# Layer 0's modulation by narrow float32 matmuls on TensorE, with another order of its weight tiles

## The chip, the core and the metric

The kernel runs on one core of one Trainium2 chip. The metric is the device time of one execution in microseconds; the runs of a kernel are given by their median. Times inside an execution are counted from the start of the profile's span.

## What is computed

Two layers on 256 tokens of width 1024. A condition vector c gives six vectors per layer (shift, scale and gate, twice); layer 0's are called SH1, SC1, G1, SH2, SC2, G2 here.

```python
cond = jax.nn.silu(c)
for l in range(DEPTH):
    mod = (cond @ w_ada[l] + b_ada[l])[:, None, :]
    sh1, sc1, g1, sh2, sc2, g2 = jnp.split(mod, N_MOD, axis=-1)
    h = rms_norm(x, norm1_g[l]) * (1.0 + sc1) + sh1
    proj = h @ w_in[l]
    ...
    y = rms_norm(y, jnp.ones((MIX_WIDTH // 2,), jnp.float32)).reshape(B, S, MIX_WIDTH) * mix_norm_g[l]
    x = x + g1 * (y @ w_out[l])
    h2 = rms_norm(x, norm2_g[l]) * (1.0 + sc2) + sh2
    x = x + g2 * peer_ffn(h2, peer_wq[l], peer_subkeys[l], peer_u[l], peer_v[l])
```

Between proj and y stand a pooling over windows and a sliding-window attention with normed queries and keys. `w_ada[l]` is 1024 x 6144 in float32, so each of the six vectors takes eight tiles of 128 x 1024 (512 KB).

## The kernel before

A layer has a mixer (`mixer`) and an expert part (`peer`). All weights come as tiles of 128 x 1024 float32 through one list, `items`, in the order of their use. `Stream` loads them on SP's queue (line 81), up to nine items ahead, into five buffers `rawt`, or for items marked so into the five buffers `hlt` of the splits. A load waits until the last reader of its buffer is done, and the queue is in order: what stands behind a waiting load waits too. Tiles of the large products are split into two float16 parts, the first by ScalarE (line 86), the second by VectorE (line 87).

The framework's scheduler puts each engine's instructions in an order when the program is built. `high_priority` and `issue_after` in the code shift that order.

Modulation of layer 0, before: `ada_step` takes a tile and accumulates cond[k] * tile in a [128, 1024] buffer on VectorE (lines 285 and 287). For G1 ScalarE scales the tile in its buffer (line 281) and GpSimd adds it (line 283). After eight tiles a product with ones sums over the partitions: `ada_cols` gives columns (line 261, eight matmuls), the gate's row is spread over all partitions by line 298. SC1 and SH1 stand first in `items`, then the ten tiles of w_in, then G1, w_out, SC2 and SH2 mixed.

The mixer of layer 0: row factors of x's norm (line 373 and `rsqrt`, lines 231 to 236), turns of x on TensorE by a diagonal of the factors (line 357 makes the diagonal, line 360 turns, four per PSUM tile), scale and shift (line 387), split into `hbuf` (lines 351, 352). Then the projection with w_in (lines 319 and 309; line 478 sums squares for the Q/K norm, line 500 spreads its factors), scores (516), probabilities turned (544), attention product (554), pooling (595 to 609). `y_half` norms each half of y and turns it (line 360 again). The output projection `mm_v` (line 327) multiplies y's two float16 parts with w_out's: six matmuls of 512 columns for each of eight slices and two token tiles, 96 in all. `residuals` multiplies by the gate, adds to x and starts the second norm; its turns come last, and behind them the first query product of the expert part (line 319).

PSUM has eight banks: two `mm`, four `acc`, two `g`. The output projection's two token tiles need two `acc` banks each.

Of the kernel before, what the change touches and what calls it, by code (L numbers as in the profile page):

```python
# [23 lines left out]
L = 2  # L24
# [21 lines left out]
class Arena:  # L46
    """Hands out column ranges of one float32 tile."""
# [15 lines left out]
class Stream:  # L63
    """Weight tiles [128, 1024] in the order of their use; loads and splits run ahead.  An item with a
    fourth field is loaded into a buffer of the splits."""
# [36 lines left out]
    def get(self, kind):  # L102
        """The next tile: (hi, lo), or the raw tile where the item has no scale."""
        i = self.at
        assert self.items[i][2] == kind, (self.items[i][2], kind)
        self._dma(i + self.ad)
        self._conv(i + self.ac)
        self.at += 1
        return self.ct.pop(i) if self.items[i][1] is not None else self.rt.pop(i)

    def advance(self, ahead=None):
        """Splits that were held back by limit."""
        self.limit = len(self.items)
        self._conv(self.at + (self.ac if ahead is None else ahead))
# [6 lines left out]
def trunk(ctx, tc, ins, out):  # L121
# [56 lines left out]
    def spread(main, bg, lo, hi):  # L178
        """bg spread evenly between main[lo:hi]."""
# [11 lines left out]

    items = []
    items += ada_rows(0, SC1) + ada_rows(0, SH1)
    items += conv_items(ins["win"][0], 10, None, "pre")
    vend = [0, 0]
    late = [t + (True,) for t in ada_rows(0, SC2)]
    for n, pair in enumerate(zip(ada_rows(0, G1), conv_items(ins["wout"][0], 8, None, "pre"))):
        items += [*pair, late[n]] if n < NSC else pair
    for n, t in enumerate(ada_rows(0, SH2)):
        items += [t, late[n]] if n >= NSC else [t]  # L200
# [39 lines left out]
    def load_exp_tables():  # L240
        """The set with ln and exp, behind the last activation that needs another one."""
# [7 lines left out]
    def mod_finish(l, c, src, j0, n):  # L249
        """mod columns from c*W: + bias, and for the scales (1 + .) * norm gain."""  # L250
# [51 lines left out]

    def mm_u(pt, w, hi, lo):
        """pt[128 columns of w, T] = w^T h over the 8 slices of the contraction."""
# [7 lines left out]
    def mm_u2(ws, hi, lo):  # L312
        """Two such products side by side, so that the slices of h are wanted at half the pace."""
# [8 lines left out]
    def mm_v(acc, w, ahi, alo, first, end):  # L322
        """acc[half][128 t, 512] += a^T w for one contraction tile and one tile of tokens."""
# [12 lines left out]
    def residuals(product, accs, grow, tmp, norm, extra):  # L336
        """product(tt), which ends accs[tt], then x += grow * accs, and the norm of x."""
# [16 lines left out]
    def transposes(pts, src, r, ks, tt):  # L354
        """Slices ks of token tile tt of src, rows scaled by r, transposed into pts, two slices each."""
# [7 lines left out]
    class Norm:  # L363
        """RMS norm of x over D, affine per column, transposed and split into hhi/hlo."""
# [4 lines left out]
        def tile(self, tt):  # L369
            """The row factors of token tile tt."""  # L370
# [22 lines left out]
    def take_pre(n):  # L393
        """Splits the next n tiles of the stream into act's first columns, before their use."""
# [6 lines left out]
    # ---------------------------------------------------------------- attention  # L401
    def mixer(l, norm):
# [36 lines left out]
        if l == 0:  # L439
            norm = Norm()  # L440
            rs = [norm.tile(tt) for tt in range(2)]
            for n in range(TAT):
                ada_step(None, None, acc_a if n < 8 else grow1)
            with tc.issue_after(last["ada"]):
                ada_cols(0, SC1, acc_a, pacc())
                for tt in range(2):
                    norm.turn(tt, rs[tt])
            for _ in range(16 - TAT):
                ada_step(pacc, None, grow1)
# [36 lines left out]
        # q: chunk c holds head c (partitions 0-63) and head 4+c (64-127)  # L486
# [75 lines left out]
        # pooling: the channel mix first, then the window means less the token, a banded product  # L562
# [11 lines left out]
        def y_half(h):  # L574
            """Group norm of one half of y, transposed, scaled and split."""
# [38 lines left out]
        if l == 0:  # L614
            acch = act[:, PRE:PRE + 1024]
            st.limit = st.at + 31
            nh = 0
            while st.at <= st.limit:
                if st.kind() == "pre":
                    take_pre(1)  # L620
                elif st.kind()[2] == G1:
                    ada_step(pmm, {G1: grow1}, grow1, True)
                elif st.kind()[2] == SH2:
                    ada_step(None, None, acch, nh < NPOOL)
                    nh += 1
                else:
                    ada_step(None)
# [5 lines left out]
        for k in range(4):  # L633
            w = pre.pop(0)
            for tt in range(2):
                mm_v(accs[tt], w, hhi[:, k, tok[tt]], hlo[:, k, tok[tt]], k == 0, False)
        ws = [pre.pop(0) for _ in range(4)]
        st.advance(4)

        def rest(tt):  # L640
            for k in range(4, 8):
                mm_v(accs[tt], ws[k - 4], hhi[:, k, tok[tt]], hlo[:, k, tok[tt]], False, k == 7)

        def extra():
            if l == 0:
                ada_cols(0, SH2, acch, pacc())
                ada_cols(0, SC2, acc_a, pacc())
# [5 lines left out]
    # ---------------------------------------------------------------- experts  # L653

    def peer(l):
# [16 lines left out]
        def picks():  # L672
            """Top-k and what follows from it, in steps of about a microsecond of the vector engine."""
# [31 lines left out]
            # gates: softmax of the picked scores, the first of which is the largest  # L705
# [3 lines left out]
            # candidate number -> (a, b)  # L709
# [48 lines left out]
        def gates():  # L758
            """act *= gate matrix, for expert columns [64 r, 64 r + 64), 8 tokens at a time."""
# [30 lines left out]
        # queries and key scores  # L790
# [45 lines left out]
        # product with V  # L836
# [57 lines left out]
def layout(inputs):  # L894
    """Host side: the inputs laid out for contiguous loads, and constants of the shapes."""
# [5 lines left out]
    def u_like(w):  # L901
        """[L, 1024, n*128] -> [L, n, 128 p, 8 k * 128 c]"""
# [3 lines left out]
    def colform(b):  # L906
        """[L, m*128] -> [128, L, m]"""
# [62 lines left out]
```

## Time and profile before

| | us |
|---|---|
| runs, median of 3 | 1781.52 |
| runs, lowest and highest | 1780.1, 1783.76 |
| profiled execution, span | 1780.2 |
| TensorE busy in it | 1705.0 |
| VectorE busy in it | 1436.6 |
| ScalarE busy in it | 852.5 |

The profile gives the span, from the first to the last instruction of one execution; the runs are whole device times, and the profiled execution has no other time of its own than its span. The mean granted clock of TensorE over the span is 0.985. The views name an instruction by its line, engine, operation, output tile and input tiles. A float32 matmul appears as two passes, so counts of float32 groups are twice those of the code. The modelled end of a matmul lies behind the start of the next one, so the distance of starts tells the pace.

### The profile page before, as it was taken

What the parts mean: (1) busy time and instruction counts of PE and PEld (TensorE: products, weight loads), DVE (VectorE), ACT (ScalarE), POOL (GpSimd) and SP (SyncE); (2) the same over time, 40 slices, a digit from 0 to 9 for tenths busy, and PEclk for the clock granted to TensorE, in tenths of its full rate; (3) what the DMA queues carried; (4) which work ended last, traced back from release to release, by engine and by line L of the source; (5) the groups of instructions that cost most, each with busy time, mean ns of one, the idle gap of its engine ahead of it and who ended that gap; (6) DMA issues with size and microseconds to landing.
All of it is one profiled execution on the core that took longest, in us unless ns stands there. A gap on an engine that the chain in (4) does not pass through costs nothing.

```text
span 1780.2 us, 33654 instructions
## 1 busy us (share of the span) xinstructions
PE 1705.0 (96%) x13524; PEld 1212.5 (68%) x13524; DVE 1436.6 (81%) x2587; ACT 852.5 (48%) x1146; POOL 29.2 (2%) x26
## 2 busy tenths in 40 slices
PE   4999989999999999999999998999999999999998
PEld 3758868999997455444458697888999845454443
DVE  6797999578889999877867499945888899986664
ACT  3645544544444444445656353545444444445543
POOL 0210000000000000000000000000000000000000
PEclk9989999999999999999999999999999999999999
DMA  8773456776665555778844144565555555556773
GB/s 315 285 277 120 168 196 220 264 241 207 222 220 187 187 190 199 257 259 314 315 155 154 36 152 163 180 220 201 187 181 188 186 181 183 185 189 213 227 227 126
DMA packets 100190, 364.04 MB, mean 204 GB/s; under 512 B 11680, under 2 KB 11696, under 8 KB 99648
## 3 DMA queue, kind: packets, MB, share of 16 engines
q1 hardware_dynamic: 99648, 361.29, 59.0%
q8 instruction: 106, 1.74, 0.4%
q0 software_dynamic: 384, 0.58, 0.1%
q14 instruction: 52, 0.43, 0.1%
HBM read 360.78 MB, written 1.05 MB: 203 GB/s over the span
## 4 chain that ended last, share of the span: by engine, by line
PE 81%; DVE 13%; DMA 2%; ACT 2%; issue 2%; SPq 0%; DVEq 0%; ACTq 0%
PE acc L327 38%; PE mm L309 34%; DVE hlt L87 4%; PE g L778 2%; PE g L780 2%; DVE act L670 1%; DVE act L668 1%; DVE act L667 1%; DVE act L669 1%; PE acc L319 1%; DMA rawt<-in_wq_dram 1%; DVE act L666 1%; DMA rawt<-in_adar_dram 1%; PE acc L516 1%; PE g L554 1%
## 5 line engine op out<-in xcount | busy, mean ns | idle before, releaser
L309 PE MATMUL mm<-hbuf,hlt 128*128 128x256 f16 x6816 | 767.5, 273 | 20.6 <-ACT act L828 11.1
L86 ACT ACTIVATE hlt<-rawt 128x1024 f16<-128x1024 f32 x544 | 571.4, 1052 | 439.9 <-PE acc L327 179.9
L87 DVE SCALAR_TENSOR_TENSOR hlt<-rawt,hlt 128x1024 f16<-128x1024 f32 x544 | 660.9, 1219 | 122.5 <-ACT hlt L86 117.9
L309 PEld LDWEIGHTS <-hlt 128*128 128x128 f16 x6816 | 662.8, 98 | 102.3 <-DVE hlt L87 13.4
L327 PE MATMUL acc<-hlt,hbuf 128*128 128x512 f16 x3072 | 674.4, 379 | 5.4 <-ACT hbuf L853 5.4
L327 PEld LDWEIGHTS <-hbuf 128*128 128x128 f16 x3264 | 314.9, 98 | 379.8 <-ACT hbuf L853 5.9
L828 ACT ACTIVATE act<-mm 128x512 f32<-128x512 f32 x128 | 76.4, 597 | 174.4 <-PE mm L309 174.4
L853 ACT ACTIVATE hbuf<-act 128x512 f16<-128x512 f32 x128 | 79.0, 626 | 101.4 <-PE acc L327 101.1
L287 DVE SCALAR_TENSOR_TENSOR acc_a<-rawt,cond,acc_a 128x1024 f32<-128x1024 f32 x59 | 75.6, 1282 | 51.1 <-DMA rawt<-in_adar_dram 50.8
L854 DVE TENSOR_TENSOR hbuf<-act,hbuf 128x512 f16<-128x512 f32 x128 | 87.7, 689 | 31.8 <-ACT hbuf L853 31.8
L768 DVE TENSOR_TENSOR lt<-iot,pk 128x1024 f16<-128x1024 f16 x128 | 87.5, 684 | 1.4 <-ACT pk L753 1.4
L783 DVE TENSOR_TENSOR act<-act,g 128x512 f32<-128x512 f32 x128 | 87.0, 680 | 1.7 <-PE g L780 1.7
L774 DVE TENSOR_TENSOR rl<-rt,pk 128x512 f16<-128x512 f16 x128 | 53.8, 421 | 33.7 <-PE g L780 33.1
L778 PE MATMUL g<-rl,lt 128*128 128x64 f16 x1024 | 78.3, 193 | 0.0
L780 PE MATMUL g<-rh,lt 128*128 128x64 f16 x1024 | 78.2, 193 | 0.0
L778 PEld LDWEIGHTS <-lt 128*128 128x128 f16 x1024 | 71.1, 97 | 8.0
L780 PEld LDWEIGHTS <-lt 128*128 128x128 f16 x1024 | 66.3, 97 | 8.0
L87 DVE SCALAR_TENSOR_TENSOR act<-rawt,act 128x1024 f16<-128x1024 f32 x36 | 46.7, 1305 | 19.8 <-ACT act L86 19.8
L770 DVE TENSOR_TENSOR rt<-iot,pk 128x512 f16<-128x512 f16 x128 | 54.2, 424 | 3.9
L86 ACT ACTIVATE act<-rawt 128x1024 f16<-128x1024 f32 x36 | 37.7, 1058 | 39.9 <-DMA rawt<-in_win_dram 31.8
L773 DVE TENSOR_TENSOR rh<-rt,pk 128x512 f16<-128x512 f16 x128 | 53.5, 418 | 0.1
L309 PE MATMUL mm<-hbuf,act 128*128 128x256 f16 x384 | 47.1, 276 | 0.0
(182 smaller groups left out, 911.0 us busy)
## 6 DMA issues: line engine op xcount, KB each, us to landing
rawt<-in_u_dram SPq DMA_DIRECT2D x256, 512.0 KB, 3.9
rawt<-in_v_dram SPq DMA_DIRECT2D x256, 512.0 KB, 3.9
rawt<-in_adar_dram SPq DMA_DIRECT2D x88, 512.0 KB, 4.4
rawt<-in_wq_dram SPq DMA_DIRECT2D x32, 512.0 KB, 4.6
rawt<-in_win_dram SPq DMA_DIRECT2D x20, 512.0 KB, 4.9
rawt<-in_wout_dram SPq DMA_DIRECT2D x16, 512.0 KB, 5.1
hlt<-in_adar_dram SPq DMA_DIRECT2D x8, 512.0 KB, 7.6
act<-in_msk_dram SPq DMA_DIRECT2D x2, 1024.0 KB, 7.9
```

Source lines behind the costliest of these rows:

```text
L86: self.nc.scalar.activation(hi, r, AF.Copy, scale=scale)
L87: self.nc.vector.scalar_tensor_tensor(lo, in0=r, scalar=scale, in1=hi, op0=ALU.mult, op1=ALU.subtract)
L287: last["ada"] = dve.scalar_tensor_tensor(acc, in0=wt, scalar=sc, in1=acc, op0=ALU.mult, op1=ALU.add).ins
L309: pe.matmul(pt, lhsT=a[:, k], rhs=b[:, k], start=n == 0, stop=n == 23)
L327: last["mm"] = pe.matmul(acc[h], lhsT=a, rhs=b[:, h * 512:(h + 1) * 512], start=first and n == 0, stop=end and n == 2).ins
L768: dve.tensor_tensor(out=lt, in0=iot.unsqueeze(1).to_broadcast([P, 4, 128, 2]), in1=pv[0].to_broadcast([P, 4, 128, 2]), op=ALU.is_equal)
L778: pe.matmul(g3[:, t], lhsT=lt[:, t // 2, :, t % 2], rhs=rl[:, t // 2, :, t % 2], start=True, stop=False)
L780: pe.matmul(g3[:, t], lhsT=lt[:, t // 2, :, t % 2], rhs=rh[:, t // 2, :, t % 2], start=False, stop=True)
L783: dve.tensor_tensor(out=av, in0=av, in1=g3.rearrange("p t i -> p i t"), op=ALU.mult)
L828: act_e.activation(act[:, ip_ * 512:(ip_ + 1) * 512], pt, AF.Gelu, scale=1.0 / WS)
L853: tabs.append(act_e.activation(ahi, src, AF.Copy))
L854: dve.tensor_tensor(out=alo, in0=src, in1=ahi, op=ALU.subtract)
```

## The change

Layer 0's SC1, SH1, SC2, SH2 and G1 leave `ada_step`. `mod_mm` multiplies each tile on TensorE in float32: cond's column k, copied to 32 columns (`condb`), stands as weights, and the tile's two halves of 512 columns stream through. A product with 32 output rows takes one of four groups of 32 columns of the array and writes 32 partitions of a PSUM bank: SC in the first two groups, SH in the other two, so one bank holds both vectors. Eight tiles add up in PSUM. `mod_cols` copies the bank, turns the rows into columns with four small matmuls and finishes as before; `mod_grow` adds the bias row and spreads the gate over all partitions with `selb`.

In `items` SC1 and SH1 alternate; behind w_in come eight triples of SC2, SH2 and w_out, then G1's eight tiles, of which the even ones are loaded into `hlt` buffers. The first norm's turns stand behind ten of the first sixteen tiles. The projection of layer 0 is written token tile by token tile: half of tile 0's slices, then the rest of tile 0, then all of tile 1. Layer 1 keeps its sums as before.

```diff
+    def paired(c0, c1):
+        return [t for pair in zip(ada_rows(0, c0), ada_rows(0, c1)) for t in pair]
+
     items = []
-    items += ada_rows(0, SC1) + ada_rows(0, SH1)
+    items += paired(SC1, SH1)
     items += conv_items(ins["win"][0], 10, None, "pre")
     vend = [0, 0]
-    late = [t + (True,) for t in ada_rows(0, SC2)]
-    for n, pair in enumerate(zip(ada_rows(0, G1), conv_items(ins["wout"][0], 8, None, "pre"))):
-        items += [*pair, late[n]] if n < NSC else pair
-    for n, t in enumerate(ada_rows(0, SH2)):
-        items += [t, late[n]] if n >= NSC else [t]
+    for n, pair in enumerate(zip(ada_rows(0, SC2), ada_rows(0, SH2), conv_items(ins["wout"][0], 8, None, "pre"))):
+        items += [pair[0] + (True,), pair[1], pair[2]]
+    items += [t + (n % 2 == 0,) if n % 2 == 0 else t for n, t in enumerate(ada_rows(0, G1))]
...
+    condb = act[:, PRE + 512:PRE + 768].rearrange("p (k m) -> p k m", k=8)
+    selb = act[:, PRE + 768:PRE + 1024].rearrange("p (h m) -> p h m", h=2)
+
+    def mod_mm(bank, q):
+        kind = st.kind()
+        _, l, c = kind
+        wt = st.get(kind)
+        k = ada_at.get((l, c), 0)
+        ada_at[(l, c)] = k + 1
+        for h in range(2):
+            o = 32 * (q + h)
+            last["mod"] = pe.matmul(bank[o:o + 32, :], lhsT=condb[:, k], rhs=wt[:, h * 512:(h + 1) * 512],
+                                    start=k == 0, stop=k == 7).ins
+
+    def mod_cols(cs, bank, rows):
+
+        act_e.copy(rows, bank)
+        pt = pacc()
+        for s in range(4):
+            pe.matmul(pt[:, s * 4:s * 4 + 4], lhsT=rows[:, s * 128:(s + 1) * 128], rhs=ident[:, 0:128:32],
+                      start=True, stop=True)
...
+    def mod_grow(bank, bias, rows, g):
+
+        dve.tensor_tensor(out=rows[0:64], in0=bank[0:64, :], in1=bias[0:64], op=ALU.add)
+        for h in range(2):
+            pt = pg()
+            pe.matmul(pt, lhsT=selb[0:64, h], rhs=rows[0:64], start=True, stop=True)
+            act_e.activation(g[:, h * 512:(h + 1) * 512], pt, AF.Copy, scale=GROW[G1])
...
-            for n in range(TAT):
-                ada_step(None, None, acc_a if n < 8 else grow1)
-            with tc.issue_after(last["ada"]):
-                ada_cols(0, SC1, acc_a, pacc())
+            bank = pacc()
+            for n in range(10):
+                mod_mm(bank, n % 2 * 2)
+            with tc.issue_after(last["mod"]):
                 for tt in range(2):
                     norm.turn(tt, rs[tt])
-            for _ in range(16 - TAT):
-                ada_step(pacc, None, grow1)
+            for n in range(6):
+                mod_mm(bank, n % 2 * 2)
+            mod_cols((SC1, SH1), bank, grow1[:, :512])
...
-            while st.at <= st.limit:
-                if st.kind() == "pre":
-                    take_pre(1)
-                elif st.kind()[2] == G1:
-                    ada_step(pmm, {G1: grow1}, grow1, True)
-                elif st.kind()[2] == SH2:
-                    ada_step(None, None, acch, nh < NPOOL)
-                    nh += 1
-                else:
-                    ada_step(None)
+            bank = pacc()
+            for _ in range(8):
+                mod_mm(bank, 0)
+                mod_mm(bank, 2)
+                take_pre(1)
+            mod_cols((SC2, SH2), bank, acc_a[:, :512])
+            bank = pacc()
+            for _ in range(8):
+                mod_mm(bank, 0)
+            mod_grow(bank, bias, acc_a[:, 512:], grow1)
...
-        for k in range(4):
-            w = pre.pop(0)
-            for tt in range(2):
-                mm_v(accs[tt], w, hhi[:, k, tok[tt]], hlo[:, k, tok[tt]], k == 0, False)
-        ws = [pre.pop(0) for _ in range(4)]
+        ws = [pre.pop(0) for _ in range(8)]
+
+        def product(tt, ks):
+            for k in ks:
+                mm_v(accs[tt], ws[k], hhi[:, k, tok[tt]], hlo[:, k, tok[tt]], k == 0, k == 7)
+
+        for tt in range(2 - (l == 0)):
+            product(tt, range(4))
...
         def rest(tt):
-            for k in range(4, 8):
-                mm_v(accs[tt], ws[k - 4], hhi[:, k, tok[tt]], hlo[:, k, tok[tt]], False, k == 7)
+            product(tt, range(4 * (l == 1 or tt == 0), 8))
```

The order of TensorE's instructions around y's turns, before: line 554 is the attention product of the last tokens, 360 the turns of y (`x2` stands for two matmuls), 327 the output projection.

```order
L544 MATMUL g<-cst,act 128x128 x12
L554 MATMUL g<-act 128x64 x16
L360 MATMUL mm<-act 128x128 x2
L360 MATMUL g<-act 128x128 x2
L360 MATMUL mm<-act 128x128 x2
L360 MATMUL g<-act 128x128 x2
L327 LDWEIGHTS hbuf
L327 MATMUL acc<-act,hbuf 128x512
```

The same place of the changed kernel, whose lines are 593 for the turned probabilities, 603 for the attention product, 401 for the turns of y and 317 for the tile products of `mod_mm` (`hlt` are tiles of SC2, `rawt` of SH2).

```order
L593 MATMUL g<-cst,act 128x128 x8
L317 MATMUL acc<-hlt,act 32x512
L603 MATMUL g<-act 128x64 x16
L317 MATMUL acc<-hlt,act 32x512
L317 MATMUL acc<-rawt,act 32x512 x2
L317 MATMUL acc<-hlt,act 32x512
L401 MATMUL mm<-act 128x128 x2
L401 MATMUL g<-act 128x128 x2
...
L401 MATMUL g<-act 128x128 x2
L317 MATMUL acc<-hlt,act 32x512
L317 MATMUL acc<-rawt,act 32x512 x2
```

The tiles S0 and H0 of SC2 and SH2 and half of S1 stand ahead of y's 16 turns, the other half of S1 and all later tiles behind them; the output projection, which began behind the first eight turns, now begins behind all tiles of SC2 and SH2.

SP's queue in the changed kernel at the same part of the program, with the engine whose work each load waits for (`hlt<-in_adar` are SC2's tiles, `rawt<-in_adar` SH2's, `wout` the output weights; DMAHW is an earlier load).

```order
L81 DMA rawt<-in_wout_dram 128x1024 [waits DMAHW7_49,PE_49]
L81 DMA hlt<-in_adar_dram 128x1024 [waits DMAHW0_49]
L81 DMA hlt<-in_adar_dram 128x1024 [waits PE_49]
L81 DMA rawt<-in_adar_dram 128x1024 [waits DMAHW2_49,PE_49]
L81 DMA rawt<-in_wout_dram 128x1024 [waits DMAHW3_49,PE_49]
L81 DMA rawt<-in_adar_dram 128x1024 [waits DMAHW4_49,PE_49]
L81 DMA rawt<-in_wout_dram 128x1024 [waits DMAHW6_49,PE_49]
```

The same of the kernel before:

```order
L81 DMA rawt<-in_adar_dram 128x1024 [waits DMAHW0_49,DVE_49]
L81 DMA rawt<-in_wout_dram 128x1024 [waits DMAHW1_49,Pool_49]
L81 DMA rawt<-in_adar_dram 128x1024 [waits DMAHW2_49,Pool_49]
L81 DMA rawt<-in_wout_dram 128x1024 [waits DMAHW3_49,DVE_49]
L81 DMA hlt<-in_adar_dram 128x1024 [waits DMAHW4_49]
```

The loads waited for VectorE and GpSimd and now wait for TensorE. The third load of the changed queue goes into the buffer of S1 and waits for S1's second product, the one that stands behind y's turns; 16 tiles of SC2, SH2, w_out and G1 are that load and those behind it.

TensorE at the end of the gate in the changed kernel; line 368 is the output projection, 341 the two products of `mod_grow`.

```order
L317 MATMUL acc<-rawt,act 32x512 x2
L368 LDWEIGHTS hbuf
L368 MATMUL acc<-act,hbuf 128x512
L368 LDWEIGHTS hbuf
L368 MATMUL acc<-act,hbuf 128x512
L368 LDWEIGHTS hbuf
L368 MATMUL acc<-act,hbuf 128x512
L368 LDWEIGHTS hbuf
L368 MATMUL acc<-act,hbuf 128x512
L341 MATMUL g<-acc_a,act 128x512 x2
L368 LDWEIGHTS hbuf
L368 MATMUL acc<-act,hbuf 128x512
```

26 of the projection's 96 products stand between the gate's tiles and ahead of `mod_grow`'s two, and 70 behind these; before, the gate's spread (line 298) stood between the turns of y's second half, with all of the projection but 17 products behind it.

## Rows read from the trace of the kernel before

**Rows 1.** The page: span, and shares of the last chain by engine.

```profile
span 1780.2 us, 33654 instructions
...
PE 81%; DVE 13%; DMA 2%; ACT 2%; issue 2%; SPq 0%; DVEq 0%; ACTq 0%
```

**Rows 2.** Timeline, 96 to 160 us: start, us, engine, line, operation.

```profile
108.83 0.61 PE L360 MATMUL g<-act 128*128 128x128 f32 x4
...
110.14 17.21 PE L327 MATMUL acc<-act,hbuf 128*128 128x512 f16 x79
...
142.04 0.38 PE L319 MATMUL acc<-hbuf,hlt 128*128 128x256 f16 x2
```

**Rows 3.** Chain of waits, layer 0, last row layer 1: start, us, what.

```profile
3.33 9.27 DMA x_sb<-in_x_dram
...
32.55 1.96 PE acc L261 x16
...
34.73 1.02 ACT act L387 x2
...
64.31 0.68 PE g L500 x4
...
89.20 6.33 PE g L554 x32
...
136.95 0.85 PE g L360 x4
...
974.98 0.45 PE g L360 x4
```

**Rows 4.** Windows: busy of PE, PEld, DVE, ACT, POOL; clock, DMA share, GB/s.

```profile
15.00:20.00 5.00, 0.00 (x0) 0.00 (x0) 4.80 (x13) 1.24 (x6) 0.00 (x0) 1.00 1.03 411
...
75.00:80.00 5.00, 5.00 (x44) 4.38 (x43) 3.54 (x10) 4.15 (x15) 0.95 (x1) 1.00 0.04 16
...
90.00:95.00 5.00, 5.00 (x26) 5.00 (x26) 4.98 (x12) 3.79 (x8) 3.06 (x2) 0.51 0.96 314
...
135.00:140.00 5.00, 4.24 (x20) 4.27 (x21) 1.65 (x9) 1.22 (x4) 0.00 (x0) 0.50 0.09 38
```

**Rows 5.** Chain of waits, 780 to 830 us: float32 products of 512 columns.

```profile
787.63 1.72 PE mm L298 x4
```

**Rows 6.** Timeline of TensorE at 66.3 us: the score product.

```profile
66.06 0.93 PE L516 MATMUL acc<-act 64*128 64x128 f32 x7
```

**Rows 7.** The page, DMA issues: KB each, us from issue to landing.

```profile
rawt<-in_u_dram SPq DMA_DIRECT2D x256, 512.0 KB, 3.9
```

**Rows 8.** Timeline of TensorE: layer 0's first projection product, then layer 1's mixer.

```profile
36.26 3.44 PE L319 MATMUL acc<-hbuf,act 128*128 128x256 f16 x14 [1.77 <-DVE hbuf L351]
...
924.78 0.63 PE L319 MATMUL acc<-hbuf,act 128*128 128x256 f16 x2
...
925.42 5.65 PE L319 MATMUL acc<-hbuf,act 128*128 128x256 f16 x46
...
980.76 0.61 PE L360 MATMUL g<-act 128*128 128x128 f32 x4
...
981.20 18.73 PE L327 MATMUL acc<-act,hbuf 128*128 128x512 f16 x86
...
1008.36 0.38 PE L319 MATMUL acc<-hbuf,hlt 128*128 128x256 f16 x2
```

**Rows 9.** Groups by line, 55 to 110 us: busy us, mean ns, idle before.

```profile
L281 ACT ACTIVATE rawt<-rawt,cond 128x1024 f32<-128x1024 f32 x7 | 8.0, 1142 | 1.3 <-DMA rawt<-in_adar_dram 1.3
L287 DVE SCALAR_TENSOR_TENSOR acc_a<-hlt,cond,acc_a 128x1024 f32<-128x1024 f32 x6 | 7.8, 1296 | 0.0
...
L357 DVE TENSOR_SCALAR act<-cst,y_r 128x128 f32<-128x128 f32 x4 | 6.2, 1548 | 0.0
```

**Rows 10.** Timeline of VectorE's last step and TensorE's product, Q/K norm.

```profile
61.63 2.21 DVE L236 SCALAR_TENSOR_TENSOR act<-rs_t,rs_y 128x20 f32<-128x20 f32 x1
...
64.31 0.68 PE L500 MATMUL g<-cst,act 128*128 128x128 f32 x4 [2.58 <-DVE act L496]
```

More of the change, by code (lines that the diff above doesn't have):

```diff
@@ L301, in trunk @@
     GROW = {G1: 1.0 / WS, G2: 1.0 / (VS * GS)}
+    condb = act[:, PRE + 512:PRE + 768].rearrange("p (k m) -> p k m", k=8)
[16 more added lines that the diff above has]
+                      start=True, stop=True)
+        pv = pt[:, 0:16].rearrange("p (s q) -> p q s", q=4)
+        for n, c in enumerate(cs):
+            o = mod[:, 0, SLOT[c]]
+            dve.tensor_tensor(out=o.rearrange("p (q s) -> p q s", q=2), in0=pv[:, 2 * n:2 * n + 2],
+                              in1=cols[:, 0, c * 8:c * 8 + 8].rearrange("p (q s) -> p q s", q=2), op=ALU.add)
+            if c in GAIN:
+                dve.scalar_tensor_tensor(o, in0=o, scalar=1.0, in1=cols[:, 0, GAIN[c]:GAIN[c] + 8],
+                                         op0=ALU.add, op1=ALU.mult)
+    def mod_grow(bank, bias, rows, g):
[4 more added lines that the diff above has]
+            act_e.activation(g[:, h * 512:(h + 1) * 512], pt, AF.Copy, scale=GROW[G1])
     def mm_u(pt, w, hi, lo):
@@ L439, in mixer @@
         if l == 0:
+            dve.tensor_copy(condb, cond.unsqueeze(2).to_broadcast([P, 8, 32]))
+            bias = act[:, PRE:PRE + 512]
+            nc.gpsimd.memset(bias, 0.0)
+            for h in range(2):
+                nc.gpsimd.dma_start(bias[32 * h:32 * h + 1, :], ins["brow"][0, 0][:, h * 512:(h + 1) * 512])
             norm = Norm()
             rs = [norm.tile(tt) for tt in range(2)]
-            for n in range(TAT):
-                ada_step(None, None, acc_a if n < 8 else grow1)
-            with tc.issue_after(last["ada"]):
-                ada_cols(0, SC1, acc_a, pacc())
+            bank = pacc()
+            for n in range(10):
+                mod_mm(bank, n % 2 * 2)
+            with tc.issue_after(last["mod"]):
                 for tt in range(2):
                     norm.turn(tt, rs[tt])
-            for _ in range(16 - TAT):
-                ada_step(pacc, None, grow1)
+            for n in range(6):
+                mod_mm(bank, n % 2 * 2)
+            mod_cols((SC1, SH1), bank, grow1[:, :512])
+            for h in range(2):
+                dve.tensor_copy(selb[:, h], ident[:, 32 * h:32 * h + 1].to_broadcast([P, 128]))
             take_pre(2)
@@ L614, in mixer @@
         if l == 0:
-            acch = act[:, PRE:PRE + 1024]
             st.limit = st.at + 31
-            nh = 0
-            while st.at <= st.limit:
-                if st.kind() == "pre":
-                    take_pre(1)
-                elif st.kind()[2] == G1:
-                    ada_step(pmm, {G1: grow1}, grow1, True)
-                elif st.kind()[2] == SH2:
-                    ada_step(None, None, acch, nh < NPOOL)
-                    nh += 1
-                else:
-                    ada_step(None)
+            bank = pacc()
[8 more added lines that the diff above has]
+            mod_grow(bank, bias, acc_a[:, 512:], grow1)
         else:
@@ L632, in mixer @@
         tok = [slice(0, 128), slice(128, 256)]
-        for k in range(4):
-            w = pre.pop(0)
-            for tt in range(2):
-                mm_v(accs[tt], w, hhi[:, k, tok[tt]], hlo[:, k, tok[tt]], k == 0, False)
-        ws = [pre.pop(0) for _ in range(4)]
+        ws = [pre.pop(0) for _ in range(8)]
[4 more added lines that the diff above has]
+            product(tt, range(4))
         st.advance(4)
         def rest(tt):
-            for k in range(4, 8):
-                mm_v(accs[tt], ws[k - 4], hhi[:, k, tok[tt]], hlo[:, k, tok[tt]], False, k == 7)
+            product(tt, range(4 * (l == 1 or tt == 0), 8))
         def extra():
-            if l == 0:
-                ada_cols(0, SH2, acch, pacc())
-                ada_cols(0, SC2, acc_a, pacc())
+            pass
         norm = Norm()
```

## The prediction

> **What bounds the kernel now.** The page comes first: TensorE carries most of the chain that ended last and VectorE a good tenth [rows 1]. Most of TensorE's share is the expert products, which the change leaves alone. So only layer 0's mixer counts, from the start to the first query product at 142.04 us [rows 2]; whatever moves that product moves the end one for one, because behind it both kernels issue the same work.
>
> The chain of waits inside that stretch is read next [rows 3]. It runs through three things. First the VectorE accumulation of SC1 and SH1, which ends in the ones-product at 32.55 and lets the first normalized slice start at 34.73. Then the Q/K norm product at 64.31 and the 32 passes of the attention product at 89.20. Then the turns of y, the last of which ends at 108.83 + 0.61 = 109.44 [rows 2], and the output projection: 79 products up to 127.35. The projection already runs while the last modulation tiles come in. The norm behind it costs 14.7 us (127.35 to 142.04), four products of it 0.85 us apart as at 136.95, which is the lower of TensorE's two clock levels (granted clock 0.50 there).
>
> Last the windows [rows 4]: the weight stream moves 411 GB/s when free, that is 0.524 MB in **1.28 us a tile**, but 16 GB/s at 75 to 80 us. It waits for buffers, and the tiles missed there are caught up beside y's turns and the projection (314 GB/s at 90 to 95).
>
> **First stage (SC1, SH1).** Removed: 16 accumulations on VectorE and both ones-products. Added: 32 narrow float32 products. A float32 product of 512 columns took 0.86 us (four passes in 1.72) [rows 5]. A tile needs two, on different columns of the array. No row shows column groups. The nearest row is the score product, whose passes stand on two halves of the rows: 7 passes in 0.93 us [rows 6], while one alone costs 0.21 at that level, so pairs overlap. I take overlap, 0.86 a tile; without it 1.72. The tenth tile lands, at 1.28 a tile behind x and the first four (12.60 [rows 3]), at 20.3 and is multiplied by 21.2. Sixteen turns stand next, eight groups of four passes at 0.45 (layer 1) to 0.85 us (at 136.95) [rows 3], 3.6 to 6.8; with the middle, 26.4. Six tiles at 0.86: 31.6. The last tile's buffer is freed only by the eleventh product (27.3), so it lands 3.9 later [rows 7] and is multiplied at 32.1. A copy, four small products and two VectorE steps take about 2 us by the ones-product's 1.96: 34.1, against 34.73, closer than these steps can be told. **No change**; -2.4 with the turns at full clock, +7 with tile products at half clock (1.72 a tile: the tenth at 23 to 24, the last six +5).
>
> **Projection to y's turns.** From the first projection product to y's last turn layer 0 takes 36.26 to 109.44, 73.2 us. Layer 1 does the same with no modulation work: 924.78 to 981.37, **56.6 us** [rows 8]. Layer 0 also loses about 3 us to the lower clock at its start: 14 passes in 3.44 us there, 46 in 5.65 in layer 1 [rows 8]. With VectorE free of the six accumulations of 1.30 us and the four row-factor products that were stretched to 1.55 [rows 9], and with the 2.58 us wait before the Q/K norm gone (the last VectorE step but one ahead of it, L236, took 2.21 beside an accumulation) [rows 10], I expect layer 1's pace: 36.26 + 56.6 + 3 = 95.9. By pieces it comes out alike: 64.31 - 2.2 = 62.1; + 24.9 to the attention product, less 1.5 and 1.1 for one accumulation and one scaling on that path = 84.4; + 6.3 at half clock; + 1.7 for four narrow products queued here; + 3.5 of turns: 95.9. **Y = 95.9**, 13.5 earlier than before. Bounds: 91 (first stage -2.4, full clock throughout) to 103 (VectorE's rows stay stretched, turns at half clock).
>
> **What the queue does then.** The order says that half of S1 and everything behind it stands after y's last turn on TensorE, and SP's queue holds the load into that buffer. Every later tile of S, H, W and the whole gate is behind it: 16 tiles that go out only after Y. Before, VectorE and GpSimd released those buffers, so that they came during 85 to 110 us. Now: first landing 3.9 us after issue [rows 7], 15 more at 1.28: 95.9 + 3.9 + 19.2 = **119.0** for the last gate tile. Work beside it hides: 9 copies and splits for W, the S and H products (0.86 of 1.28 us), the 26 projection products that stand between gate tiles. In the eight gate slots TensorE has 0.86 + 3.25 x 0.218 = 1.57 a tile, against 1.28: +2.4, 121.4. Then four projection products 0.9, the row add 0.65 (half the columns of an accumulation of 1.30 [rows 9]), two broadcasts 1.7 [rows 5]: 124.7.
>
> **Projection by token tile.** 96 products; 70 are left behind the gate, since token tile 1's accumulators wait for the gate's bank. At layer 1's 0.218 (18.73 for 86) [rows 8] that is 15.3: 140.0. Before, the projection was nearly over when the gate was. What is hidden again is the norm of token tile 0 (48 products, 10.5 us). The tail is layer 1's, 999.93 to 1008.36 = 8.4 instead of 14.7, because TensorE comes to it without a pause: 148.4.
>
> **The sum.** 148.4 - 142.04 = **+6.4 us**. Terms: first stage 0, y's turns -13.5, tail -6.3, and between Y and the end of the projection 44.1 us instead of 17.9, +26.2. Not costed, since they lie beside the tile stream: bias load and memset on GpSimd, the broadcast copies of cond and the selectors on VectorE, the columns of SC2 and SH2 (wanted only at the norm's end; uncovered 2 us), and layer 1's projection, which keeps its order. The profiled span is 1780.2, 0.07% under the median 1781.52, so the shift carries over: **1787.9 us**.
>
> **A rule weighed.** The score product's passes overlap on different rows, 0.93 us for seven [rows 6]. The Trainium skill, page "TensorE: Matmul & The Clock Gate", Part 3, "What overlaps and what doesn't", says that a weight load overlaps products in flight only where the row groups differ; all column groups here share theirs, so by that rule the pair would be serial, and the time the third rival's 1815. The same page's table of packings lists three column groups at 2.38 times one; by that the pair overlaps, and the sum stays at 1787.9. No row here settles it.
>
> **Rivals.** (1) *Faster.* VectorE's relief and the clock pay more than layer 1's pace: accumulations 7.8 us, row factors 6.2, L236 2.2 [rows 9, 10], all on the chain; 3 us each of lower clock at the first projection products and the attention product; 2.4 in the first stage. Together 24.6 of 109.4, Y = 84.8: 11.1 below my Y, less the 6.4: **1777**. It decides at Y below 85.9, since 0.2% is 3.6 us, about what a measurement can tell from no change. For it: those rows of VectorE stand in the way of the two norms. Against: layer 1 has none of them and needs 56.6 all the same. (2) *Within 0.2%.* The first stage gains 2.4 and TensorE then stays at full clock: Y = 91 to 93, +1.5 to +3.5, **1784**. For it: TensorE now has work where the window of 15 to 20 shows none [rows 4]. (3) *Column groups are serial*: 1.72 us a tile, above the stream's 1.28. First stage: 2.5 for the first ten tiles, 5.2 for the six behind the turns (0.44 and 0.86 a tile over the main case). Before Y: two tiles, +1.7. After Y TensorE sets the pace: 14 tiles of S and H at 1.72 and eight gate slots at 1.72 + 0.71 make 43.5 instead of 25.5, +18.0. Sum +27.4 on the main case: **1815**. For it: the order puts one column group's pass behind the other's with the weights changed between. Against: the score product's overlap. (4) *Each change between narrow and whole-array products waits for the array to empty.* Four passes of a turn last 0.61 in the timeline while the next four start 0.45 later [rows 3, 8], so a change would cost the tail of 0.16; 16 changes in the gate make +2.6, **1790.5**. Nothing in the rows speaks for it. The Trainium skill's "TensorEngine Tiling (Array Packing)", Key Properties, says that a change of tiling mode drains TensorE, which is this rival; no run here shows it.
>
> **Chances.** Main 0.40 (+4 to +9), rival 1 0.11, rival 2 0.25, rival 3 0.12, rival 4 0.12. Slower: 0.40 + 0.12 + 0.12 = 0.64; same 0.25; faster 0.11. The range leaves out about half of rival 1 and most of rival 3: 1777.5 to 1800; the likeliest case alone 1785.5 to 1791.
>
> **What would show it.** Starts of the narrow passes: a tile every 0.86 (overlap) or 1.72. The first normalized slice near 34.7; y's last turn near 96; the load into S1's buffer issued right behind it, and then 16 tiles at 411 GB/s; the last gate tile near 119; 70 projection products behind the broadcasts up to 140; the first query product at 148; layer 1 as before. I am wrong if Y comes below 90, if the loads after Y go out earlier than its end, or if TensorE spends over 1.6 us a gate tile.

## The result, and the profile after

The changed kernel takes 1795.55 us (median of four runs, 1790.69 to 1796.73) against 1782.19 for the kernel before: ratio 1.0059, interval 1.0041 to 1.0078. By the ratio it is slower by about 10.5 us; the two medians lie 13.4 us apart. 1787.9 was forecast, with a range of 1777.5 to 1800 and 1785.5 to 1791 for the main case alone.

The profiled execution spans 1793.1 us, 12.9 us more than in [rows 1]. The page's first line:

```profile
span 1793.1 us, 33801 instructions
```

The first query product stands at 153.67 us, 11.6 behind that of [rows 2], and behind it only 1.3 us are added. So the loss lies where it was looked for. The chain of waits of the changed kernel from the first normalized slice to that product (start us, us, what; line 317 is a tile product, 368 the output projection, 401 a turn):

```profile
33.33 0.56 ACT act L428
...
85.00 3.72 PE g L603 x32
...
93.48 3.60 PE acc L317 x31
...
97.47 8.35 DMA hlt<-in_adar_dram
...
105.86 1.24 PE acc L317 x4
107.14 1.95 PE acc L317 x4
...
109.74 1.87 PE acc L325 x8
111.61 1.85 PE acc L317 x4
...
117.81 0.98 PE acc L317 x4
118.79 0.76 PE acc L368 x3
...
128.44 1.91 PE g L341 x4
130.35 15.01 PE acc L368 x69
```

The reader is to see four stretches. The first slice starts at 33.33 and not at 34.73 [rows 3]. Behind y's turns TensorE multiplies the tiles that are there (3.60 us), then the chain is a load, 8.35 us. From 105.86 to 128.44 it is TensorE, but for one copy of 0.59 us by ScalarE at 109.11, and at first it is slow: 1.95 us for four narrow passes at 107.14 and 1.85 at 111.61, where four take 0.98 at 117.81. Then come the gate's spread, 70 projection products in 15.0 us, and the norm.

The windows show the stream and the clock in these stretches (busy time of PE, PEld, DVE, ACT, POOL; clock; DMA share; GB/s):

```profile
70.00:75.00 5.00, 5.00 (x43) 4.43 (x42) 4.89 (x12) 2.63 (x12) 0.00 (x0) 1.00 0.02 10
...
100.00:105.00 5.00, 1.72 (x12) 0.14 (x4) 1.72 (x2) 2.11 (x2) 0.00 (x0) 1.00 1.02 412
105.00:110.00 5.00, 3.42 (x10) 0.59 (x10) 0.73 (x1) 0.90 (x2) 0.00 (x0) 0.66 1.03 415
110.00:115.00 5.00, 5.00 (x16) 2.14 (x16) 1.50 (x4) 0.65 (x1) 0.00 (x0) 0.50 1.02 409
```

From 70 to 75 us the stream moves 10 GB/s, as it stood still in [rows 4] at 75; from 100 to 115 it is full, and TensorE, busy for only 1.72 of 5 us at 100, is granted 0.66 and then 0.50, the lower of its two levels, just when the last pair of SC2 and SH2 tiles has come. (The gate's tiles still land then; the chain doesn't wait for them.)

SP's timeline shows when the queue stood (us, time on the queue, loads), and VectorE's has two splits of w_out:

```profile
61.35 0.33 SPq L81 DMA_DIRECT2D hlt<-in_adar_dram  x1
76.28 0.33 SPq L81 DMA_DIRECT2D rawt<-in_wout_dram  x1
86.22 0.33 SPq L81 DMA_DIRECT2D rawt<-in_adar_dram  x1
...
90.14 4.67 SPq L81 DMA_DIRECT2D hlt<-in_adar_dram  x2
```

```profile
74.98 1.22 DVE L87 SCALAR_TENSOR_TENSOR act<-rawt,act 128x1024 f16<-128x1024 f32 x1
...
84.98 1.22 DVE L87 SCALAR_TENSOR_TENSOR act<-rawt,act 128x1024 f16<-128x1024 f32 x1
```

No load goes out between 61.35 and 76.28, nor from there to 86.22. Both times the next load follows right behind a split of a w_out tile that stands between attention's steps in VectorE's order, so the stand of 70 to 75 us is not the tile products' doing. They hold the queue only behind that: by the waits of the trace 3.1 us ahead of the load at 89.75, then 4.0 us. The pair at 90.14 is S5 and S6; the second waited on the queue, most of those 4.67 us, until S1's second product, right behind y's last turn, had freed its buffer. The timeline of TensorE has that turn, tile products behind it, and the first query product:

```profile
92.87 0.61 PE L401 MATMUL g<-act 128*128 128x128 f32 x4
...
95.15 0.60 PE L317 MATMUL acc<-rawt,act 128*32 128x512 f32 x2
95.17 1.00 PE L317 MATMUL acc<-hlt,act 128*32 128x512 f32 x2
95.58 0.60 PE L317 MATMUL acc<-rawt,act 128*32 128x512 f32 x2
...
153.67 0.63 PE L360 MATMUL acc<-hbuf,hlt 128*128 128x256 f16 x2
```

The last turn ends at 92.87 + 0.61 = 93.48. Two passes of an SH2 tile start with two of an SC2 tile 0.02 us behind, and the next ones 0.43 later: four column groups work at once, and a tile costs 0.43 us as long as SC2 and SH2 tiles overlap.

### The profile page after: what moved, and what is told of

Same layout as the page of the kernel before. It is cut to its first block, busy times and chain, and to the rows that moved or that the text cites. A ratio compares the mean times of both kernels' runs of the same rounds, so it can differ in the third digit from the quotient of the medians.

```text
span 1793.1 us, 33801 instructions
## 1 busy us (share of the span) xinstructions
PE 1727.3 (96%) x13636; PEld 1203.9 (67%) x13636; DVE 1393.4 (78%) x2559; ACT 845.6 (47%) x1140; POOL 9.4 (1%) x19
## 3 DMA queue, kind: packets, MB, share of 16 engines
q8 instruction: 106, 1.74, 0.4%
HBM read 360.78 MB, written 1.05 MB: 202 GB/s over the span
## 4 chain that ended last, share of the span: by engine, by line
PE 82%; DVE 12%; DMA 3%; issue 1%; ACT 1%; SPq 0%; DVEq 0%; ACTq 0%
PE acc L368 39%; PE mm L350 33%; DVE hlt L87 4%; DMA rawt<-in_adar_dram 2%; PE g L827 2%; PE g L825 2%; PE acc L360 1%; DVE act L717 1%; PE acc L317 1%; DVE act L715 1%; DVE act L714 1%; DVE act L716 1%; DVE act L713 1%; PE acc L565 1%; PE g L603 1%
## 5 line engine op out<-in xcount | busy, mean ns | idle before, releaser
L288 DVE SCALAR_TENSOR_TENSOR acc_a<-rawt,cond,acc_a 128x1024 f32<-128x1024 f32 x52 | 66.7, 1283 | 53.0 <-DMA rawt<-in_adar_dram 52.9
```

What stands on the lines that cost most here:

```text
L288: last["ada"] = dve.scalar_tensor_tensor(acc, in0=wt, scalar=sc, in1=acc, op0=ALU.mult, op1=ALU.add).ins
```

## The experiments

Ratios are to the kernel before on the same chip; its medians there were 1784.1 to 1784.7. Each "first query product" is to be read against 142.04 before and 153.67 in the changed kernel.

**1. The first stage alone.**

```diff
-    for n, pair in enumerate(zip(ada_rows(0, SC2), ada_rows(0, SH2), conv_items(ins["wout"][0], 8, None, "pre"))):
-        items += [pair[0] + (True,), pair[1], pair[2]]
...
+    for n, pair in enumerate(zip(ada_rows(0, G1), conv_items(ins["wout"][0], 8, None, "pre"))):
+        items += [*pair, late[n]] if n < NSC else pair
...
+                elif st.kind()[2] == G1:
+                    ada_step(pmm, {G1: grow1}, grow1, True)
```

> Only SC1 and SH1 go to TensorE, in the changed order; the second stage, its tile order and the projection are those of before. Theory (the loss lies in the second stage): the first normalized slice starts near 33.3 us as in the changed kernel, the projection gains 0.5 us or so, and the time is 1780 to 1783, within 3 us of before. Rival (the loss begins in the first stage, since the win tiles come in no earlier and their splits are late): the query/key stage is later by 3 us or more and the time is 1786 or more.

1787.41 us, ratio 1.0029 (1.0007 to 1.0052); first slice 32.76, y's turns to 108.36, first query product 143.26. The chain (line 545 is the Q/K norm's product, 301 the gate's spread, 370 the output projection):

```profile
64.72 0.68 PE g L545 x4
...
108.36 1.72 PE mm L301 x4
110.08 20.72 PE acc L370 x96
```

The median lies 2.8 us above before's: within the theory's 3 us, but outside its 1780 to 1783 and in the rival's range of 1786 or more, and the interval does not hold a ratio of 1. The rival's mechanism isn't seen, since the Q/K norm's product comes 0.4 us later than in [rows 3] and not 3. The first stage gains 2 us at the slice; 1.1 of them are left at y's last turn and none at the first query product. In this order all 96 projection products lie behind the turns and not 79 [rows 2], 20.72 us for 17.21, and the norm behind them takes 12.5 us for 14.7. The profiled execution (1783.41) is the second fastest of ten, so this places 1.2 us and not the whole distance of the medians.

**2. The second stage alone.**

```diff
-    items += paired(SC1, SH1)
+    items += ada_rows(0, SC1) + ada_rows(0, SH1)
...
-            for n in range(10):
-                mod_mm(bank, n % 2 * 2)
...
+            for n in range(TAT):
+                ada_step(None, None, acc_a if n < 8 else grow1)
...
```

> Only the second stage (SC2, SH2, G1 on TensorE, gate last, projection token tile by token tile); SC1 and SH1 stay on VectorE as before. Theory: all of the loss is here, y's last turn at 93 to 96, TensorE waits for tiles behind it, first query product near 154, time 1792 to 1796. Rival (first stage): at most 1788.

1793.79 us, ratio 1.0049 (1.0032 to 1.0066); first query product 149.15, where the theory had 154. Its time holds, 1792 to 1796: most of the loss is here.

```profile
93.45 4.11 PE acc L317 x32
...
97.96 8.19 DMA hlt<-in_adar_dram
...
109.43 1.05 PE acc L325 x8
110.48 0.98 PE acc L317 x4
...
124.81 1.91 PE g L341 x4
```

Y's last turn ends at 93.45, as in the changed kernel, although the first slice starts only at 36.07. With run 1's 108.36 that says that nearly all of the gain at y's turns comes from the second stage's sums, which VectorE and GpSimd no longer do. The load at the end of the wait takes about as long as in the changed kernel, 8.19 us and 8.35. But TensorE was back at the upper level by 109: the column products took 1.05 us and not 1.87, four passes 0.98 and not 1.85, and the gate's spread began at 124.81 and not at 128.44. From the columns on it is the same work, so some 3.3 us of the changed kernel's loss are the lower clock, by one execution of each.

**3. The gate's bank.**

```diff
-            bank = pacc()
+            bank = pmm()
             for _ in range(8):
                 mod_mm(bank, 0)
...
-        for tt in range(2 - (l == 0)):
+        for tt in range(2):
             product(tt, range(4))
...
```

> The changed kernel with the gate's PSUM bank taken from the two mm banks, so that the products of token tile 1 need not wait for the gate; the order has 37 projection products ahead of the gate's spread instead of 26, 59 instead of 70 behind it. Theory A (TensorE is the bound behind y's turns, the tiles set when the gate ends): 11 products of 0.218 us go into waits or not, -2.4 us at most, time 1792 to 1795. Rival (the 48 products of token tile 1 behind the gate's bank are the loss): -8 us or more, 1787 or less.

1796.45 us, ratio 1.0063 (1.0040 to 1.0086); first query product 154.04. Nothing is gained; the time lies 1.5 us above theory A's 1792 to 1795.

```profile
111.77 4.71 PE acc L368 x11
...
131.32 1.91 PE g L341 x4
133.23 12.64 PE acc L368 x58
```

Eleven products stand ahead of the first gate tile now, at 0.43 us each, which is the lower clock, and push the spread from 128.44 to 131.32; behind it are 59 and not 70. The sum is the same. The rival falls: token tile 1 behind the gate's bank was no loss, since TensorE had no gap there to fill.

**4. The gate's tiles first.**

```diff
...
-        items += [pair[0] + (True,), pair[1], pair[2]]
...
+    for n, pair in enumerate(zip(ada_rows(0, G1), conv_items(ins["wout"][0], 8, None, "pre"))):
+        items += [pair[0] + (True,) if n % 2 == 0 else pair[0], pair[1]]
+    for n, pair in enumerate(zip(ada_rows(0, SC2), ada_rows(0, SH2))):
+        items += [pair[0] + (True,), pair[1]]
...
```

(The gate also takes an `mm` bank, and SC2 and SH2 are multiplied between the projection's products.)

> The changed kernel with G1 and w_out ahead of SC2 and SH2 in the stream, the gate in an mm bank, all 96 projection products free of the gate's bank, and SC2 and SH2 multiplied between projection products. Theory (the order of the tiles is the loss, not the move to TensorE): most of G1 and w_out are in when y's turns end near 92, the gate is done near 101, TensorE does not wait for tiles behind it, first query product at 138 to 144, time 1778 to 1784. Rival (the move itself costs, 24 tiles of 0.43 to 0.98 us on TensorE behind the turns, and the lower clock): first query product at 147 or later, time 1787 or more.

1790.25 us, ratio 1.0025 (1.0011 to 1.0038); first query product 150.79. The profiled execution (1796.59) is the slowest of its eight. The order took back part of the loss, but the expected 138 to 144 and 1778 to 1784 were missed, and both numbers of the rival were met (147 or later, 1787 or more). The trace adds a reason that neither had:

```profile
96.46 6.99 PE mm L318 x32
...
106.33 9.60 PE acc L369 x44
...
132.14 3.19 DMA rawt<-in_wq_dram
...
144.27 0.21 DVE act L399
```

The gate was done early, as expected: eight tiles together took 6.99 us and 44 projection products 9.60 (0.218 each). In the changed kernel a gate slot holds four narrow passes (0.98) and three projection products (0.76), 1.74 against 0.874 + 3 x 0.218 = 1.53 here. The difference, 0.21 us a slot, goes with two changes between narrow and whole products, so about 0.1 each. The last rows show what was new: VectorE's order had five splits of wq ahead of the norm's row factor at 144.27, and the first of them waited for its load until 135.33. TensorE had been done with the projection at 138.9.

**5. SC2 and SH2 ahead of y's turns.**

```diff
+        if l == 0:
+            st.limit = st.at + 31
+            bank = pacc()
+            for _ in range(8):
+                mod_mm(bank, 0)
+                mod_mm(bank, 2)
+                take_pre(1)
         apply(1)
         with tc.high_priority():
```

(The same lines are taken out behind `y_half(1)`.)

> The changed kernel with the products of SC2 and SH2 written ahead of the last attention product, so that their buffers come free before y's turns; gate last as before. Theory (the stream that waits behind y's turns is the larger part of the loss): the 5 us windows between 70 and 95 us move 200 GB/s or more instead of 10 to 105, y's turns end 6 to 12 us later because up to 14 tiles of 0.4 to 1.0 us stand ahead of them, the gate's spread ends near 120 instead of 130.3, first query product at 144 to 148. Rival (TensorE is full there, so that each tile product moved forward moves the turns by as much): gate's spread at 128 or later, first query product at 152 or later.

One time, 1783.23 us; span 1781.5, first query product 142.87. The stream and the chain:

```profile
70.00:75.00 5.00, 5.00 (x42) 3.83 (x39) 4.92 (x10) 2.76 (x10) 0.00 (x0) 1.00 0.00 0
...
85.00:90.00 5.00, 4.89 (x34) 2.54 (x30) 1.98 (x6) 1.17 (x3) 0.00 (x0) 1.00 0.96 367
```

```profile
83.11 4.84 DMA rawt<-in_adar_dram
...
104.20 0.98 PE acc L317 x4
...
120.44 15.01 PE acc L368 x69
```

The stream is busy from 85 us on and not from 95. It did nothing at 70 to 75, which the theory had wrong: the queue waited there, as in the changed kernel, for VectorE's split of a w_out tile (no load goes out from 60.32 to 74.99), and TensorE waited at 83 for a tile in its order. The turns end at 101.4, 8 us later, yet the gate's spread ends at 120.44, 10 us earlier, and the lower clock is not met: the first gate tile at 104.20 takes 0.98. So this run moves two things at once, the loads and the place of the lower clock.

**6. The same, timed.**

> The run with SC2 and SH2 ahead of y's turns once more, timed in rounds. Theory (the stream that waits behind y's turns was the loss): ratio to before 0.998 to 1.002, first query product within 1.5 us of 142.9 and so level with before. Rival (that one time was a chance): ratio 1.003 or more.

1788.38 us, ratio 1.0024 (1.0015 to 1.0034). Its profiled execution has the first query product at 145.27 and a span of 1789.5. So neither expectation is met (at most 1.002 and 144.4, or 1.003 and more): the one time was at the fast end, and the edit takes back 0.35% of the 0.59%, some 6 us, not all.

**7. Another order on the same engine.** G1 and w_out first as in 4, then

```diff
+                mod_mm(bank, n % 2 * 2, n < 2, n > 5)
...
+            bank = pmm()
+            for _ in range(5):
+                mod_mm(bank, 0)
+                mod_mm(bank, 2)
...
+                for _ in range(3):
+                    mod_mm(bank, 0)
+                    mod_mm(bank, 2)
+                mod_cols((SC2, SH2), bank, acc_a[:, :512])
+                st.advance(4)
```

where the first line gives gate tiles in turn to either pair of column groups (the sum of both is taken in the spread), five pairs of tiles stand in the middle of the projection and three behind it.

> A version from the readings so far: G1 and w_out ahead of SC2 and SH2, gate tiles on alternating pairs of column groups so that two of them overlap, the projection free of the gate's bank, five pairs of SC2 and SH2 tiles behind half of the projection, three behind its end, and the splits of wq held until then. Theory: gate 4 to 5 us instead of the 7.0 in the run with the gate first, no wait for tiles of more than 3 us behind y's turns, the projection ends near 127, the norm behind it takes 9 to 10 us and not 12, first query product at 136 to 140, time 1776 to 1782. Rival (the norm's steps of VectorE, held up by splits, set the end whatever TensorE does): first query product at 145 or later, 1786 or more.

1782.67 us, ratio 0.9992 (0.9981 to 1.0004); first query product 139.86. As fast as before; the product is where it was expected, and the time is 0.7 us above the expected 1776 to 1782. Ten tiles take 4.43 us in a row, 0.44 each. What stands in the way is again VectorE, whose split of a late wq tile holds the row factor until 136.46:

```profile
110.93 4.43 PE mm L318 x40
...
128.99 6.21 DMA rawt<-in_wq_dram
...
135.23 1.23 DVE hlt L87
136.46 0.21 DVE act L399
```

**8. The early tiles with the gate together.** Run 5 with the gate's eight tiles in two pairs of groups, behind half of the projection of both token tiles.

```diff
+            with tc.issue_after(last["mm"]):
+                bank = pmm()
+                for n in range(8):
+                    mod_mm(bank, n % 2 * 2, n < 2, n > 5)
+                mod_grow(bank, bias, acc_a[:, 512:], grow1)
```

> The run with SC2 and SH2 ahead of y's turns, and besides the gate in an mm bank, its tiles on alternating pairs of column groups and together, behind the first half of the projection of both token tiles. Theory (what is left of the loss there is TensorE time in the gate slots and token tile 1 behind the gate): eight gate tiles take 3.5 to 4 us together instead of 14.3 with 26 products between, projection ends near 131, first query product at 137 to 141, time 1776 to 1780. Rival (the splits of wq on VectorE, which stand ahead of the residual of token tile 0, wait for loads that the gate's buffers hold): first query product at 142 or later, no better than before.

1781.43 us, ratio 0.9986 (0.9971 to 1.0002); first query product 138.04. The chain (the gate's 32 passes run from 114.69 on):

```profile
104.38 10.38 PE acc L368 x48
114.76 2.76 PE mm L317 x24
...
117.54 4.24 DMA rawt<-in_wq_dram
```

The gate takes 3.5 us with 24 of its passes in 2.76, as expected, where it took 14.3 with 26 products between in run 5; the norm then waits for VectorE, which is held up by a load of wq. The theory's 137 to 141 is met, its 1776 to 1780 is missed by 1.4 us, and the interval holds a ratio of 1; the rival's mechanism is seen as well.

**9. Splits behind the norm.** In 7 and in 8 the first splits of wq are called behind the norm:

```diff
-                st.advance(4)
...
         residuals(rest, accs, grow1, tmp, norm, extra)
+        if l == 0:
+            with tc.issue_after(last["dve"]):
+                st.advance(1)
```

> The reordered version with the first splits of wq held behind the second norm's row factors. Theory (VectorE waited in its order on a wq tile that came late, with the norm's steps behind it): no wait of VectorE on wq between 125 and 136, both row factors by 132, first query product at 136 to 139, 1.5 to 4 us earlier than the 140 of that version. Rival (wq's landing sets the time, wherever its split stands): first query product at 140 or later.

1780.70 us, ratio 0.9974 (0.9960 to 0.9988); first query product 136.25. This is the fastest version, 0.26% below before and, by the two ratios, about 0.85% below the changed kernel.

```profile
95.00 3.57 PE mm L318 x32
...
111.01 4.43 PE mm L318 x40
...
132.17 0.04 DVE act L399
```

The gate's 32 passes take 3.57 us, the tile products behind it 4.43, and both row factors are done by 132.2.

> The run with early SC2 and SH2 tiles and the gate's eight tiles together, with the splits of wq called behind the norm; three of them still stand ahead of token tile 0's row factor in VectorE's order. Theory: projection ends near 131, tail 8 to 9 us, first query product at 138 to 141. Rival (the splits still wait for their tiles): as the run before it, 142 or later.

1782.72 us, ratio 0.9986 (0.9970 to 1.0002); first query product 139.55, as expected (138 to 141) and no better than run 8: three splits still stand ahead of token tile 0's row factor, and the chain has a load of wq of 6.0 us there.

## Why the forecast was right in direction, and where its sum was off

The direction was right and the time lies in the stated range, but above the main case's own 1785.5 to 1791: the trace's shift of the first query product is 11.6 us, the forecast's was 6.4. One of the forecast's own signs of being wrong is met: "over 1.6 us a gate tile", measured 1.74 at the upper clock and 2.1 in the mean (16.83 us for eight). Term by term:

- **First stage, 0.** Measured 1.4 early at the slice, and lost again: the first projection product stands at 36.48, against 36.26 in [rows 8]. Run 1 has it alone and no gain at the end either.
- **Y = 95.9.** Measured 93.48. The reading by layer 1's pace was 2.4 us too late. TensorE ran the attention product at the upper clock (3.72 us at 85.00 in the chain), which the sum had at 6.3. That the relief of VectorE brings the turns forward was right (runs 1 and 2).
- **The queue.** Right: S6's load waits for y's turns, and the 16 tiles come behind it at 410 GB/s. Run 5 shows that this place counts: only the tile products are moved, and the spread ends 10 us earlier though the turns end 8 us later; what the lower clock cost in the changed kernel is part of the 10. Unsaid in the forecast: until 86.22 the queue stood for VectorE's splits of w_out, not for TensorE's tile products.
- **The gate slots, the step that was mis-sized.** A gate slot is a gate tile with the projection products behind it. The sum said "In the eight gate slots TensorE has 0.86 + 3.25 x 0.218 = 1.57 a tile, against 1.28: +2.4, 121.4", as if TensorE took gate tiles while they landed. From Y to the spread's end it allowed 28.8 us; measured 93.48 to 130.35 = 36.9, **8.1 more**. The order has the gate behind all tiles of SC2 and SH2, for whose last pair TensorE waited until 105.86; the first gate product followed at 111.6, and eight whole slots behind it, 16.8 us, where only their excess over the stream was counted. The last gate tile's load went out at 109.10 and its product started at 126.42, so the stream no longer set the pace. Of the 8.1 about 4.5 are the lower clock, which the sum did not have there: 3.3 from the columns on (run 2 against the changed kernel), and 1.2 ahead of them by the chain's rows, 1.24 and 1.95 for what takes 0.98. 1.7 are the changes of shape (eight times 0.21, run 4); the rest, 1.9, is put down to this order only by subtraction.
- **Projection behind the gate, 15.3, and tail, 8.4.** Measured 15.0 and 8.3. The tail's size is right and its reason, "because TensorE comes to it without a pause", is not: TensorE waits 3 us ahead of the last turns and makes them at the lower clock (0.85 us a group of four), in the changed kernel as in layer 1 of the kernel before, from which the 8.4 was taken:

```profile
150.50 0.81 PE L401 MATMUL mm<-act,x_sb 128*128 128x128 f32 x4 [3.15 <-DVE act L398]
```

```profile
1004.86 1.22 PE L360 MATMUL mm<-act,x_sb 128*128 128x128 f32 x4 [3.06 <-DVE act L357]
```

In the 14.7 us of the kernel before, the chain runs through VectorE's splits of wq, such as 1.22 us at 130.26; in these two tails it does not.

The terms close: -2.4 + 8.1 - 0.4 = 5.3 over the forecast's 148.4, and the product stands at 153.67.

**The rivals.** Serial column groups (1815) are refuted by starts 0.02 us apart and 0.43 us a tile. The rule of the Trainium skill, "TensorE: Matmul & The Clock Gate", Part 3, that weight loads overlap only where row groups differ, by which they would be serial, is not borne out by this trace; the table of packings beside it (2.38 for three column groups) points the right way, and four groups here took no longer than one pass alone (0.43, [rows 5]). So the sum's 0.86 a tile was twice too much for SC2 and SH2, which cost nothing, since these products wait for tiles. The change of shape is real: 0.1 us each where I had 0.16, 1.7 us in the gate where I had 2.6; the Trainium skill, "TensorEngine Tiling (Array Packing)", Key Properties, names such a drain; the slots agree that a change costs time, though not that a drain is the cause. It was an addition to the main case and not an alternative to it. The faster rival fell because Y would have had to be 85.9. The rival within 0.2% came near its condition, Y = 91 to 93, and fell all the same, because the loss lies behind Y. That the lower clock would come back behind a wait for tiles was in no rival; it should have been, since the profile before shows it behind TensorE's other pauses (busy 3.43 of 5 us at 85, granted 0.51 at 90).

What stays open: the runs' times of the whole program differ by more than the mixer's part explains. Runs 5 and 6 are the same kernel, and between their first query product and layer 1's first projection product they take 782.6 and 787.7 us (142.87 to 925.43, 145.27 to 932.98). So the last 1 to 3 us of each ratio are not put down to a cause here. The price of the lower clock rests on single profiled executions.

## What to carry to other kernels

Moving work from one engine to another moves the release of its buffers too: look in the order for what stands ahead of the instruction that frees a buffer, and in the load queue for what stands behind that load. When a sum mixes a stream and an engine, ask where the engine's first item starts before charging only the excess; a block that starts when the stream is nearly over is paid whole. Small products on four column groups cost a quarter each if they stand together (four passes in 0.43 us), so batch them; a few whole-array products between them give part of that back, and the same work in another order made about 0.85% here.

## What the hardware showed unexpectedly

Four float32 passes on four column groups, each with 512 columns of its own and a weight load of its own, ran in the 0.43 us of one. A change between narrow and whole-array products cost about 0.1 us. After waits of 1.5 to 2.7 us for tiles between 97 and 106 us TensorE was granted 0.66, 0.50 and 0.82 in the next three windows though it was busy for 3.4 us of the first and throughout the other two; in run 2, after waits of 1.95 and 1.51 us, the lower level came at 100 to 110 (0.61 and 0.71) and was over when the gate began. There it fell in part on time in which TensorE would have waited for tiles anyway (its third wait is 0.63 us and not 2.65); in the changed kernel it fell on the gate, and cost 3.3 us more.
